# In the scan parts of a hybrid attention and RWKV-7 kernel that keep both directions in one PSUM bank, all products are issued ahead of the reads of the bank

## The chip, the cores and the metric

The kernel runs on one core of one Trainium2 chip. The metric is the time of one execution on the device in microseconds (us). The engines are TensorE (PE, its weight loads PEld), VectorE (DVE), ScalarE (ACT), GpSimd (POOL) and SyncE (SP, which issues most transfers). PSUM is the memory that TensorE writes its products to; a tile of 128 partitions by 512 float32 fills one bank of it.

## What is computed

One layer of an encoder with 2048 tokens of width 1024: a shared input projection, an attention branch (8 heads, low-rank queries and keys), a bidirectional RWKV-7 branch, gates, and a mixture of experts. The change lies in the RWKV-7 branch, a linear recurrence that runs once forward and once backward over the tokens:

```
def step(state, inp):
    r_t, w_t, k_t, v_t, a_t, b_t = inp
    sa = jnp.einsum('bhvk,bhk->bhv', state, a_t)
    state = (state * w_t[:, :, None, :] + sa[..., None] * b_t[:, :, None, :]
             + v_t[..., None] * k_t[:, :, None, :])
    return state, jnp.einsum('bhvk,bhk->bhv', state, r_t)
...
y_f = wkv7_scan(r_h, decay_h[:, :, 0], k_dir[:, :, 0], v_h, -kk, kk * a_h[:, :, 0])
y_b = fl(wkv7_scan(fl(r_h), fl(decay_h[:, :, 1]), fl(k_dir[:, :, 1]), fl(v_h),
                   fl(-kk), fl(kk * a_h[:, :, 1])))
y = y_f + y_b
```

## The kernel before, in words

The program has three phases. Phase 1 projects and prepares the operands. Phase 2, which the change touches, runs attention and both scans interleaved. Phase 3 merges the branches and runs the experts.

The scans cut the 2048 tokens into 32 chunks of 64 (index n). At step n the forward scan works on chunk n and the backward scan on chunk 31 - n; d is the direction. A chunk is worked off in parts, each a method of the class `Rwkv`, and each part's products of both directions go to the two halves of one PSUM bank:

- `products(n, d)` (L968) multiplies keys and receptances within a chunk into the bank `sa`; VectorE masks the result into the tile `stk` (L970). It has one direction to itself.
- `tokens(n, e)` (L990) transposes decayed operands through `sa`; ScalarE copies them to `bkt` (L991).
- `inner(n)` (L1003): 16 products into `sa`, 8 for each direction; VectorE masks each half into `arb` (L1004).
- `state(n)` (L1030): 16 products of the state `mv` into the bank `rec`; ScalarE copies each half to `rs` (L1031). VectorE and GpSimd make the decayed state `m0` from `mv` (L1034). Sixteen products into the bank `yy` follow (L1040).
- `solve(n)` (L1053): 16 products of `rs` with the inverted matrices `tt` into `rec`; of each half VectorE copies the lower 64 partitions back to `mv` (L1055) and ScalarE the upper 64 (L1056).
- `update(n)` (L1069): 16 products into `rec`; VectorE adds `m0` to each half in two instructions, which gives the next state `mv` (L1072). Sixteen products into `yy` follow (L1078), which ScalarE copies to `ys` (L1085).

In `inner`, `state`, `solve` and `update` the products of direction 0 come first, then the reads of its half, then the products and the reads of direction 1. The banks `sa`, `rec` and `yy` have one buffer each.

Attention works on 32 blocks (8 heads by 4 blocks of 512 queries), in four rounds v each. A round issues two times `scores` (four score tiles `s`, each three products of 128x512, L684 to L686, whose exponential ScalarE takes into `e`, L689; VectorE or GpSimd adds `e` to a sum, L694). Between these stand the products of a later block's row maxima (L664), which VectorE reduces (L665). Then comes one step of the scans, then `av` (L701: four products of `e` with the values; in the first round of a block those of the block before), then another step of the scans. So a scan part is followed by `av` in one half of the cases and by a burst of scores in the other. The tiles `s` rotate over four PSUM banks. ScalarE also casts the keys of each new head (`kh`, in the helper `split`, L498) behind the transfer that brings them.

TensorE's order in this phase is that of the code: the loop stands under `tc.manual_schedule(engines={nc.tensor.engine})`. The order on the other engines is made by the tile framework's scheduler, which also puts in the semaphores: it keeps any two engines from working on one PSUM tile at a time, halves included. Each engine works off its own queue in order.

Of the kernel before, what the change touches and what calls it, by code (L numbers as in the profile page):

```python
# [798 lines left out]
class Rwkv:  # L799
# [193 lines left out]
    def inner(self, n):  # L993

        nc = self.k.nc
        st, bk, _ = self.pair[n // 2]
        ar = self.ops[n][0] = self.p.tile([128, 2, 4, 64], F32, name="arb")
        tv = self.bank("sa").rearrange("p (q t) -> p q t", t=64)
        for d in range(2):
            c, s = self.where(n, d)  # L1000
            for g in range(4):
                for e, r, ro in self.HEADS:
                    nc.tensor.matmul(tv[r, 4 * d + g], bk[r, s, d, g, e], st[r, s, e, d, g, 1], start=True, stop=True)  # L1003
            nc.vector.tensor_tensor(ar[:, d], tv[:, 4 * d:4 * d + 4],  # L1004
                                    self.mask[:, d:d + 1, 64:128].to_broadcast([128, 4, 64]), op=OP.mult)

# [5 lines left out]
    def state(self, n):  # L1012

        k, p = self.k, self.p
        nc, Q = k.nc, self.Q
        st, _, mv = self.pair[n // 2]
        if n == 0:
            for e, r, _ in self.HEADS:
                for d in range(2):
                    nc.gpsimd.memset(mv[r, self.where(n, d)[1], e, d], 0.0)  # L1020

        m0 = self.m0 = p.tile([128, 8, 64], F32, name="m0", bufs=1)
        rs = self.rs = p.tile([128, 8, 64], F32, name="rs", bufs=1)
        t, y = self.wide("rec"), self.wide("yy")
        self.y = y
        for d in range(2):
            c, s = self.where(n, d)
            for g in range(4):
                for e, r, _ in self.HEADS:
                    nc.tensor.matmul(t[r, 4 * d + g], st[:, s, e, d, g, 0], mv[:, s, e, d, g], start=True, stop=True)  # L1030
            nc.scalar.copy(rs[:, Q[d]], t[:, Q[d]])  # L1031
            if n < 31:
                for e, r, _ in self.HEADS:
                    (nc.gpsimd if e else nc.vector).tensor_tensor(  # L1034
                        m0[r, Q[d]], mv[r, s, e, d], k.wc[r, d, :, c:c + 1].to_broadcast([64, 4, 64]), op=OP.mult)
        for d in range(2):
            c, s = self.where(n, d)
            for g in range(4):
                for e, r, _ in self.HEADS:
                    nc.tensor.matmul(y[r, 4 * d + g], st[:, s, e, d, g, 1], mv[:, s, e, d, g],  # L1040
                                     start=(d == 0 and g == 0), stop=False)

    def solve(self, n):

        nc, Q = self.k.nc, self.Q
        mv, tt = self.pair[n // 2][2], self.tt[n // 4]
        i = n % 4
        t = self.wide("rec")
        for d in range(2):
            c, s = self.where(n, d)  # L1050
            for g in range(4):
                for e, r, _ in self.HEADS:
                    nc.tensor.matmul(t[r, 4 * d + g], tt[r, d, g, i if d == 0 else 3 - i], self.rs[r, 4 * d + g],  # L1053
                                     start=True, stop=True)
            nc.vector.tensor_copy(mv[self.E, s, 0, d], t[self.E, Q[d]])  # L1055
            nc.scalar.copy(mv[self.O, s, 1, d], t[self.O, Q[d]])  # L1056

    def update(self, n):

        nc, S, Q = self.k.nc, self.k.scratch, self.Q  # L1060
        mv = self.pair[n // 2][2]
        ar, bt = self.ops.pop(n)
        if n < 31:
            t = self.wide("rec")
            for d in range(2):
                c, s = self.where(n, d)
                for g in range(4):
                    for e, r, _ in self.HEADS:
                        nc.tensor.matmul(t[r, 4 * d + g], bt[:, e, 4 * d + g], mv[:, s, e, d, g], start=True, stop=True)  # L1069
                mn, sn = self.pair[(n + 1) // 2][2], self.where(n + 1, d)[1]  # L1070
                for e, r, _ in self.HEADS:
                    nc.vector.tensor_tensor(mn[r, sn, e, d], t[r, Q[d]], self.m0[r, Q[d]], op=OP.add)  # L1072
        y = self.y
        for d in range(2):
            c, s = self.where(n, d)
            for g in range(4):
                for e, r, _ in self.HEADS:
                    nc.tensor.matmul(y[r, 4 * d + g], ar[r, d, g], mv[r, s, e, d, g], start=False,  # L1078
                                     stop=(d == 1 and g == 3))
        if n % 2 == 0:  # L1080
            self.ys = self.p.tile([128, 2, 2, 4, 64], F32, name="ys", bufs=1)
        ys = self.ys
        for d in range(2):
            c, s = self.where(n, d)
            nc.scalar.copy(ys[:, d, s], y[:, Q[d]])  # L1085
            if n % 2:
                c0 = n - 1 if d == 0 else 31 - n
                for e, r, _ in self.HEADS:
                    nc.sync.dma_start(S["y"][d, c0 * 64:c0 * 64 + 128, e * 256:e * 256 + 256]
                                      .rearrange("(c t) x -> t c x", t=64),  # L1090
                                      ys[r, d].rearrange("p s g f -> p s (g f)"))
# [839 lines left out]
```

## Time and profile before

| | us |
|---|---|
| median of 3 runs | 3733.64 (3726.69 to 3735.77) |
| the profiled execution, its own time | 3723.98 |
| its span, first to last instruction | 3722.2 |
| TensorE busy | 3297.7 |
| VectorE busy | 2590.2 |
| ScalarE busy | 1508.5 |
| GpSimd busy | 1399.6 |

The scans' products run from 1327.9 us to 2530.3 us of the span. In a profile, a group's idle time is that of its engine just before the group's instructions, and the arrow behind it names what ended the idle time. The products of a scan part are float32 and are recorded twice each, so that a half of 8 products shows as x16. The end of a product is modelled: a product that runs behind others is shown longer than it holds the engine up, so the starts of consecutive groups tell more than their lengths.

### The profile page before, as it was taken

Reading aid. Unit: us, or ns where it says so; the run is one execution under the profiler, and the core shown is the slowest. Engines: PE = TensorE matmul, PEld = TensorE weight load, DVE = VectorE, ACT = ScalarE, POOL = GpSimd, SP = SyncE. Lnnn points to the kernel's source line nnn. Section 1 sums busy time; section 2 is a strip of 40 time slices with the busy share of each in tenths; the row PEclk is TensorE's granted clock in tenths of the full one; section 3 lists DMA queues with packets and bytes.
Section 4 is the critical chain, followed back from the end, with each engine's and each line's share of the span. In section 5 each row is a group of like instructions: output and inputs, shape, how many; then the busy total and the mean of one; then the engine's idle time right before and its main releaser. Section 6 shows DMA issues by size and latency. Waiting matters only on the chain. (4 is left out here: it accounts for less than half of the span.)

```text
span 3722.2 us, 66958 instructions
## 1 busy us (share of the span) xinstructions
PE 3297.7 (89%) x25104; PEld 2447.8 (66%) x25104; DVE 2590.2 (70%) x4767; ACT 1508.5 (41%) x2866; POOL 1399.6 (38%) x1301
## 2 busy tenths in 40 slices
PE   8999999999888788888888888889699997899990
PEld 6778777777666656555565656565488886666660
DVE  6845677777987656666666666767667676678777
ACT  5322445445443333333333333334322222677762
POOL 1022232234222433444444444434433222565553
PEclk9999999999998889999999999999799998899995
DMA  5545767676554342233332332201454444788887
GB/s 174 167 154 172 214 201 206 199 199 203 193 168 148 118 116 70 65 96 93 89 94 87 90 93 74 62 18 32 130 171 137 131 143 171 260 319 325 335 330 293
DMA packets 392838, 589.71 MB, mean 158 GB/s; under 512 B 66880, under 2 KB 245184, under 8 KB 392512
## 3 DMA queue, kind: packets, MB, share of 16 engines
q1 hardware_dynamic: 380016, 546.36, 46.3%
q0 software_dynamic: 11920, 38.30, 2.7%
q8 instruction: 198, 3.24, 0.4%
q14 instruction: 128, 1.05, 0.1%
q10 hardware_dynamic: 576, 0.76, 0.1%
HBM read 380.78 MB, written 204.51 MB: 157 GB/s over the span
## 5 line engine op out<-in xcount | busy, mean ns | idle before, releaser
L145 PE MATMUL z<-hhi,wlo 128*128 128x512 f32 (+1 forms) x1184 | 469.6, 397 | 4.0 <-POOL wlo L136 4.0
L144 PE MATMUL z<-hlo,whi 128*128 128x512 f32 (+1 forms) x1184 | 471.5, 398 | 0.2 <-DVE hlo L188 0.2
L143 PE MATMUL z<-hhi,whi 128*128 128x512 f32 (+1 forms) x1184 | 469.0, 397 | 1.9 <-ACT hhi L187 1.8
L689 ACT ACTIVATE e<-s 128x512 f32<-128x512 f32 x512 | 304.4, 597 | 393.6 <-PE s L686 370.1
L694 POOL TENSOR_TENSOR acc<-acc,e 128x512 f32<-128x512 f32 x224 | 294.3, 1314 | 403.4 <-ACT e L689 399.4
L665 DVE TENSOR_REDUCE mx<-s 128x1 f32<-128x512 f32 x512 | 339.9, 683 | 82.5 <-PE s L664 80.4
L694 DVE TENSOR_TENSOR accv<-accv,e 128x512 f32<-128x512 f32 x224 | 242.3, 1082 | 41.0 <-ACT e L689 39.3
L136 POOL TENSOR_TENSOR wlo<-wraw,whi 128x1024 fp32r<-128x1024 f32 x61 | 151.4, 2483 | 308.0 <-ACT whi L135 264.1
L145 PEld LDWEIGHTS z<-hhi,wlo 128*128 128x128 f32 (+1 forms) x1184 | 222.7, 188 | 63.6 <-issue 8.8
L144 PEld LDWEIGHTS z<-hlo,whi 128*128 128x128 f32 (+1 forms) x1184 | 222.6, 188 | 56.3 <-issue 3.9
L143 PEld LDWEIGHTS z<-hhi,whi 128*128 128x128 f32 (+1 forms) x1184 | 222.5, 188 | 56.2 <-issue 3.0
L701 PE MATMUL o<-e,v 128*64 128x512 f32 x1024 | 256.4, 623 | 0.0
L498 ACT CAST wh<-wr 128x1024 fp32r<-128x1024 f32 x198 | 204.3, 1047 | 107.1 <-PE y L1632 51.5
L499 POOL TENSOR_TENSOR wl<-wr,wh 128x1024 fp32r<-128x1024 f32 x70 | 186.8, 2687 | 125.9 <-ACT wh L498 125.9
L684 PE MATMUL s<-qhi,kh 128*128 128x512 f32 x512 | 212.4, 415 | 19.8 <-ACT e L689 16.7
L499 DVE TENSOR_TENSOR wl<-wr,wh 128x1024 fp32r<-128x1024 f32 x128 | 185.5, 1455 | 63.0 <-ACT wh L498 58.5
L664 PE MATMUL s<-kh,qhi 128*128 128x512 f32 x512 | 224.0, 445 | 2.2 <-DVE mx L665 2.2
L685 PE MATMUL s<-qlo,kh 128*128 128x512 f32 x512 | 205.9, 402 | 0.0
L686 PE MATMUL s<-qhi,kl 128*128 128x512 f32 x512 | 204.9, 400 | 0.0
L970 DVE TENSOR_TENSOR stk<-sa,mask 64x512 f32<-64x512 f32 x128 | 88.2, 689 | 77.0 <-PE sa L968 75.0
L684 PEld LDWEIGHTS s<-qhi,kh 128*128 128x128 f32 x512 | 98.8, 193 | 59.0 <-ACT e L689 32.7
L664 PEld LDWEIGHTS s<-kh,qhi 128*128 128x128 f32 x512 | 100.9, 198 | 50.6 <-DVE mx L665 11.5
(484 smaller groups left out, 7896.1 us busy)
## 6 DMA issues: line engine op xcount, KB each, us to landing
wr<-w_exp SPq DMA_DIRECT2D x198, 512.0 KB
wraw<-w_in SPq DMA_DIRECT2D x61, 512.0 KB
s_ye<-ye SPq DMA_DIRECT2D x33, 512.0 KB
s_ar<-ar SPq DMA_DIRECT2D x64, 256.0 KB
s_bk<-bk SPq DMA_DIRECT2D x64, 256.0 KB
s_zg<-zo SPq DMA_DIRECT2D x64, 256.0 KB
bk<-s_bk SPq DMA_DIRECT2D x32, 512.0 KB
stk<-s_ar SPq DMA_DIRECT2D x64, 256.0 KB
```

The lines of the kernel that those rows point to most:

```text
L143: nc.tensor.matmul(t[:rows], hi[:, c, :rows], hhi[b][:, c], start=(c == 0), stop=False)
L144: nc.tensor.matmul(t[:rows], hi[:, c, :rows], hlo[b][:, c], start=False, stop=False)
L145: nc.tensor.matmul(t[:rows], lo[:, c, :rows], hhi[b][:, c], start=False, stop=(c == 7))
L499: (eng or k.nc.vector).tensor_tensor(lo, src, hi.bitcast(F32), op=OP.subtract)
L664: nc.tensor.matmul(t, B.qhi[:, i * 128:(i + 1) * 128], KT[B.h][0][b], start=True, stop=True)
L665: nc.vector.tensor_reduce(B.mx[:, i, b:b + 1], t, axis=AX.X, op=OP.max)
L684: nc.tensor.matmul(t, khi[b][:, c], B.qhi, start=True, stop=False)
L685: nc.tensor.matmul(t, khi[b][:, c], B.qlo, start=False, stop=False)
L686: nc.tensor.matmul(t, klo[b][:, c], B.qhi, start=False, stop=True)
L689: nc.scalar.activation(e, t, AF.Exp, scale=scale)
L694: eng.tensor_tensor(a, a, e, op=OP.add)
L701: nc.tensor.matmul(B.o[r], VT[B.h][:, 2 * u + i], B.e[u][i], start=(u == 0), stop=(u == NT // 2 - 1))
```

## The change

In the four parts whose bank holds both directions, the loop over the directions is cut in two: the first loop issues the 16 products, the second the reads of both halves. No instruction is added or removed. TensorE's order is the same instruction by instruction; its waits within a part are gone, and the scheduler orders the other engines anew.

```diff
@@ inner
                 for e, r, ro in self.HEADS:
                     nc.tensor.matmul(tv[r, 4 * d + g], bk[r, s, d, g, e], st[r, s, e, d, g, 1], start=True, stop=True)
+
+        for d in range(2):
             nc.vector.tensor_tensor(ar[:, d], tv[:, 4 * d:4 * d + 4],
                                     self.mask[:, d:d + 1, 64:128].to_broadcast([128, 4, 64]), op=OP.mult)
@@ state
                 for e, r, _ in self.HEADS:
                     nc.tensor.matmul(t[r, 4 * d + g], st[:, s, e, d, g, 0], mv[:, s, e, d, g], start=True, stop=True)
+        for d in range(2):
+            c, s = self.where(n, d)
             nc.scalar.copy(rs[:, Q[d]], t[:, Q[d]])
@@ solve
                     nc.tensor.matmul(t[r, 4 * d + g], tt[r, d, g, i if d == 0 else 3 - i], self.rs[r, 4 * d + g],
                                      start=True, stop=True)
+        for d in range(2):
+            c, s = self.where(n, d)
             nc.vector.tensor_copy(mv[self.E, s, 0, d], t[self.E, Q[d]])
             nc.scalar.copy(mv[self.O, s, 1, d], t[self.O, Q[d]])
@@ update
                     for e, r, _ in self.HEADS:
                         nc.tensor.matmul(t[r, 4 * d + g], bt[:, e, 4 * d + g], mv[:, s, e, d, g], start=True, stop=True)
+            for d in range(2):
                 mn, sn = self.pair[(n + 1) // 2][2], self.where(n + 1, d)[1]
                 for e, r, _ in self.HEADS:
                     nc.vector.tensor_tensor(mn[r, sn, e, d], t[r, Q[d]], self.m0[r, Q[d]], op=OP.add)
```

With the change L1004, L1031, L1053, L1055, L1056, L1069, L1072 and L1078 become L1006, L1035, L1057, L1061, L1062, L1075, L1079 and L1085.

TensorE around the update and the inner part behind it, at n = 1, before:

```order
L716 MATMUL s<-cst,acc 128x2 x3
L1069 MATMUL rec<-mv,bkt 64x64 x8
L1069 MATMUL rec<-mv,bkt 64x64 [waits DVE_49]
L1069 MATMUL rec<-mv,bkt 64x64 x7
L1078 MATMUL yy<-mv,arb 64x64 x16
L701 MATMUL o<-e,v 64x512 x4
L1003 MATMUL sa<-stk,bk 64x64 x8
L1003 MATMUL sa<-stk,bk 64x64 [waits DVE_49]
L1003 MATMUL sa<-stk,bk 64x64 x7
```

and with the change:

```order
L716 MATMUL s<-cst,acc 128x2 x3
L1075 MATMUL rec<-mv,bkt 64x64 x16
L1085 MATMUL yy<-mv,arb 64x64 x16
L701 MATMUL o<-e,v 64x512 x4
L1003 MATMUL sa<-stk,bk 64x64 x16
```

The two waits on VectorE in the middle of a part are gone, and nothing stands in another place.

VectorE around the solve part of n = 2 (`mv<-rec` is its copy of a half, L665 the maxima of a burst of scores), before:

```order
L707 TENSOR_TENSOR ob<-o,ob 64x512 [waits DMAHW1_49,Activation_49]
L1055 COPY mv<-rec 64x256 [waits PE_49]
L1055 COPY mv<-rec 64x256 [waits PE_49,Activation_49]
L665 TENSOR_REDUCE mx<-s 128x1 [waits PE_49] x3
L694 TENSOR_TENSOR accv<-accv,e 128x512 [waits DVE_49,Activation_49]
L665 TENSOR_REDUCE mx<-s 128x1 [waits PE_49]
```

and with the change:

```order
L707 TENSOR_TENSOR ob<-o,ob 64x512 [waits DMAHW1_49,Activation_49]
L1061 COPY mv<-rec 64x256 [waits PE_49]
L665 TENSOR_REDUCE mx<-s 128x1 [waits PE_49]
L1061 COPY mv<-rec 64x256 [waits Activation_49]
L665 TENSOR_REDUCE mx<-s 128x1 [waits PE_49] x2
L694 TENSOR_TENSOR accv<-accv,e 128x512 [waits DVE_49,Activation_49]
L665 TENSOR_REDUCE mx<-s 128x1 [waits PE_49]
```

The second copy no longer waits for products of its own but for ScalarE, which reads the same bank between the two, and one of the maxima has moved ahead of it.

ScalarE around the same solve part (L991 is the copy of the transposed tokens, whose products follow the solve on TensorE), before:

```order
L706 COPY ob<-o 64x512 [waits DMAHW1_49,PE_49,Pool_49]
L1056 COPY mv<-rec 64x256 [waits DVE_49]
L991 COPY bkt<-sa 128x512 [waits PE_49]
L1056 COPY mv<-rec 64x256 [waits DVE_49]
L689 ACTIVATE e<-s 128x512 [waits PE_49,Activation_49]
L689 ACTIVATE e<-s 128x512 [waits PE_49,Pool_49]
L689 ACTIVATE e<-s 128x512 [waits PE_49,Activation_49]
L689 ACTIVATE e<-s 128x512 [waits PE_49,Pool_49]
```

and with the change:

```order
L706 COPY ob<-o 64x512 [waits DMAHW1_49,PE_49,Pool_49]
L991 COPY bkt<-sa 128x512 [waits PE_49]
L1062 COPY mv<-rec 64x256 [waits DVE_49]
L689 ACTIVATE e<-s 128x512 [waits PE_49,Activation_49]
L1062 COPY mv<-rec 64x256 [waits DVE_49]
L689 ACTIVATE e<-s 128x512 [waits PE_49,Activation_49] x2
L689 ACTIVATE e<-s 128x512 [waits PE_49,Pool_49]
```

The copy L991 has moved ahead of the first of the two copies of the solve, and an exponential ahead of the second.

## Rows read from the trace of the kernel before

**Rows 1.** Windows with and without scans: busy us by engine, granted clock, DMA.

```profile
1600.00:1800.00 200.00, 175.01 (x1724) 119.68 (x1722) 132.25 (x205) 68.79 (x130) 84.56 (x83) 0.96 0.33 92
...
2560.00:2600.00 40.00, 38.88 (x173) 22.65 (x172) 33.15 (x46) 16.62 (x29) 20.12 (x17) 1.00 0.06 14
```

**Rows 2.** Waits of TensorE over the span: total us, times, longest.

```profile
PE rec L1053 <- ACT mv L1056: 46.7, 32, 4.8
PE rec L1069 <- DVE mv L1072: 46.7, 31, 2.6
PE sa L1003 <- DVE arb L1004: 26.5, 32, 3.4
PE rec L1030 <- ACT rs L1031: 17.4, 32, 0.9
PE s L684 <- ACT e L689: 16.7, 22, 3.0
...
PE s L664 <- DVE mx L665: 2.2, 4, 1.1
```

**Rows 3.** The same for TensorE's weight loads.

```profile
PEld rec L1053 <- ACT mv L1056: 51.1, 32, 4.9
PEld rec L1069 <- DVE mv L1072: 51.0, 31, 2.8
...
PEld sa L1003 <- DVE arb L1004: 30.9, 32, 3.5
...
PEld rec L1030 <- ACT rs L1031: 21.8, 32, 1.0
```

**Rows 4.** Timeline, all engines, one update part and the scores behind it.

```profile
1967.19 0.64 PE L1069 MATMUL rec<-mv,bkt 128*64 128x64 f32 x16
...
1967.87 0.88 DVE L1072 TENSOR_TENSOR mv<-rec,m 64x256 f32<-64x256 f32 x2 [1.96 <-PE rec L1069]
...
1968.80 0.69 PE L1069 MATMUL rec<-mv,bkt 128*64 128x64 f32 x16 [0.98 <-DVE mv L1072]
1969.42 1.15 PE L1078 MATMUL yy<-mv,arb 64*64 64x64 f32 x32
...
1970.44 1.18 DVE L1034 TENSOR_TENSOR m<-mv,wc 64x256 f32<-64x256 f32 x2
...
1970.88 0.48 PE L664 MATMUL s<-kh,qhi 128*128 128x512 f32 x1
...
1975.37 0.68 PE L1003 MATMUL sa<-stk,bk 64*64 64x64 f32 x16
```

**Rows 5.** Timeline of TensorE: two other bursts of scores, first and next group.

```profile
1904.81 0.51 PE L664 MATMUL s<-kh,qhi 128*128 128x512 f32 x1
...
1909.12 0.69 PE L1030 MATMUL rec<-mv,stk 128*64 128x64 f32 x16
...
1926.24 0.48 PE L664 MATMUL s<-kh,qhi 128*128 128x512 f32 x1
...
1930.21 0.69 PE L1069 MATMUL rec<-mv,bkt 128*64 128x64 f32 x16
```

**Rows 6.** Windows: the first and the last of 18 stretches at half clock.

```profile
1391.90:1395.30 3.40, 3.40 (x50) 2.57 (x46) 2.02 (x4) 0.65 (x2) 1.55 (x2) 0.50 0.02 5
2504.60:2508.00 3.40, 3.40 (x36) 2.99 (x35) 1.51 (x3) 0.65 (x2) 0.00 (x0) 0.51 0.01 2
```

**Rows 7.** Timeline of TensorE at the first of these stretches.

```profile
1391.64 0.94 PE L1069 MATMUL rec<-mv,bkt 128*64 128x64 f32 x16 [1.17 <-DVE mv L1072]
1392.51 1.97 PE L1078 MATMUL yy<-mv,arb 64*64 64x64 f32 x32
```

**Rows 8.** Groups by line, 1345:2530 (busy us, mean ns, idle before).

```profile
L991 ACT COPY bkt<-sa 128x512 f32<-128x512 f32 x62 | 36.3, 585 | 54.1 <-PE sa L990 53.5
...
L1055 DVE COPY mv<-rec 64x256 f32<-64x256 f32 x63 | 25.9, 410 | 39.0 <-PE rec L1053 39.0
...
L498 ACT CAST kh<-raw 96x512 fp32r<-96x512 f32 x24 | 14.8, 617 | 44.0 <-DMA raw<-s_krr 44.0
```

## The prediction

> **What bounds the kernel now.** I read the windows first. With scans running, TensorE is busy 175 of 200 us, VectorE 132, ScalarE 69 and GpSimd 85, at a granted clock of 0.96; in the stretch of attention behind the last scan part TensorE is busy 38.9 of 40 us at a clock of 1.00 [rows 1]. So the stage with scans, some 1,200 of 3,722 us, is TensorE's, and one eighth of it is lost to waits that attention alone does not have. The list of TensorE's waits names them: the second half of a solve waits 46.7 us in all for ScalarE's copy, that of an update 46.7 us for VectorE's sums, that of an inner part 26.5 us for the mask, that of a state part 17.4 us for the copy to `rs`. That is 137.3 us in 127 waits. The next ones on the list in this stage are small: 16.7 us for the exponential to give back a score bank, 2.2 us for a maximum [rows 2]. TensorE's order is fixed in the code, so nothing else can be put into these holes: what one costs is lost to the whole stage, and the stage is passed before phase 3 can go on.
>
> **The change, part by part.** Nothing is added or removed; what moves are waits.
>
> *The waits inside the parts.* All 127 go: the 16 products stand in one piece. In the timeline of one update the second half starts 1.61 us behind the first (1967.19 to 1968.80), while the second half hands over to the next line after 0.62 us; the idle time printed between them is 0.98 us [rows 4]. The idle of a matmul counts from a modelled end. The weight loads, which the same waits hold back, show 51.1 + 51.0 + 30.9 + 21.8 = 154.8 us [rows 3]. The gain lies between 137.3 and 154.8 us; I take 150, nearer to the loads, because a load is what has to start first.
>
> *The clock.* Between 1345 and 2530 us the trace has 18 stretches at a granted clock of half (1.2 GHz), 15 of 3.4 us and 3 of 6.8 us; the first and the last are shown [rows 6]. Sixteen of them, 14 short and 2 long, begin within 6 us of the start of one of the waits that go, of 1.2 to 4.8 us [rows 2, 7]; the other two begin behind waits for an exponential, of up to 3.0 us [rows 2]. In the first one 32 products take 1.97 us [rows 7], which take 1.15 us at full clock [rows 4]. The 16 sum to 14 x 3.4 + 2 x 6.8 = 61 us, of which half, 31 us, is lost where TensorE is busy all along. Some of it passes in idle, and a new wait can bring a stretch back: I take 22, with 0 and 31 as ends.
> The Trainium skill (TensorE: Matmul & The Clock Gate, "A second HAM failure mode: psum-queue depth-cycling") says that short idles between groups of matmuls, which come from cycling through PSUM, make the clock fall and rise again and again. The trace agrees as far as 16 of 18 stretches go. If the whole stage kept its clock by this rule, half of 71 us would come back, and the sum would be 14 us lower.
>
> *What comes instead, behind the parts.* Two engines read what TensorE has left, and now begin behind all 16 products. Where `av` follows (half of the cases), it covers them. Where a burst of scores follows, the maxima stand behind the reads in VectorE's queue, and the four score banks run out. Two bursts give the price: one behind transposed tokens takes 3.97 us (1926.24 to 1930.21), one behind `products`, a part whose reads already begin behind all of its products, 4.31 us [rows 5]: 0.34 us more. Behind an update a burst takes 4.49 us already (1970.88 to 1975.37), and one pair of sums of 0.88 us, now done inside the wait, will stand ahead of it too, with the 1.18 us of the next `m0` behind as now [rows 4]. So 16 updates at up to 0.88 us give 14 us, 16 inner parts at 0.34 give 5, and 16 solves at 0.34 give 5; the two copies of a state part are covered by the products into `yy` (1.15 us for 32, as in rows 4's update). Sum 24; between 5 (the sums covered by the `yy` products) and twice that.
>
> *The backlog.* Of the 137.3 us a part was not the read itself but an engine that was late. The least price of an update's wait is its two sums and 0.10 us of handing over, 0.98 [rows 4]; 31 of them are 30.4 of 46.7. A solve needs two copies of about 0.41 us [rows 8], one behind the other, and two hand-overs, 1.02; 32 are 32.6 of 46.7. An inner or state part needs one, 0.51: 16.3 of 26.5 and of 17.4. That leaves 16.3 + 14.1 + 10.2 + 1.1 = 42 us of lateness, which does not vanish: it meets `av` in one half of the cases and the four score banks in the other. I let a third return, 14, with 0 and 42 as ends.
>
> *The casts.* ScalarE stands 44.0 us behind transfers before it casts the keys of a new head [rows 8]; TensorE feels part of that as its 16.7 us. The transfers will not be faster, and TensorE arrives at them sooner: 8 us more, between 0 and 27 (44.0 less 16.7).
>
> *The sum.* 3724.0 (the profiled execution's own time; its span is 3722.2) - 150 - 22 + 24 + 14 + 8 = 3598. The median of the runs, 3733.6, lies 9.7 above that execution, so the forecast for the median is 3608, 3.4% less. Taking every term at its better end gives 154.8 + 31 - 5 = 181 less, 3553; at its worse end 137.3 - 48 - 42 - 27 = 20 less, 3713. Phases 1 and 3 keep their order on every engine and are costed at nothing: the first product that changes lies at 1328 us, and the last difference on any engine lies ahead of the merge.
>
> **Rivals.**
> *A. The bursts take most of it.* VectorE's 132 us of 200 [rows 1] become about 78% if the stage loses 172 of 1,200 us, and it is unevenly loaded: it is late at the end of a burst and catches up behind it. The holes that go are where it caught up. If it no longer does, each of the some 112 bursts beside the 224 scan steps pays about 0.7 us more (twice the 0.34 behind `products`): 80 us, so 3688. For it speaks that bursts already stretch from 3.97 to 4.49 us; against it that only 2.2 us of waiting for maxima stand in the list [rows 2], and that `av` lies between any two bursts.
> The Trainium skill (Perfetto Trace Analysis, "Optimizing Tensor Performance", "Matmuls") wants independent groups in different banks, so that the reads of one lie beside the products of the next. The change does the contrary within a part, and by this rule rival A, with its 3688, is the likelier one. The trace bears it out only where a burst follows, since `av` and the bursts use other banks than the part.
> *B. Nothing changes.* Each wait reappears whole at the next semaphore, for the score banks or for `sa`: 3733. For it speaks that the same engines still have to read the same halves. Against it: behind each part stands `av` or a burst, and neither uses the bank that is being read.
> *C. Slower: the alternation of VectorE and ScalarE in the solve.* With the change VectorE's second copy waits for ScalarE's first one, and ScalarE has the tokens' copy L991 (0.585 us [rows 8]) ahead of that, in all 32 solves. An engine that is stuck there keeps maxima and exponentials behind it in its queue, and TensorE runs out of score banks. It decides once a solve costs TensorE over 172 / 32 = 5.4 us; at 6 us the time is 3733.6 - 172 + 192 = 3754. The chain itself is only 4 x 0.41 + 0.59 = 2.2 us, so that would need a cast that waits for its transfer in most solves, where there are 24 casts.
>
> **How the numbers follow.** My sum 0.77, A 0.15, B 0.05, C 0.03. The range leaves C and B out and reaches into A: 3565 to 3690; the likeliest case's own is 3575 to 3645. Differences under 0.3% can't be told from no change here. Faster 0.92, same 0.05, slower 0.03.
>
> **What would show it.** Right: the four waits in rows 2 are gone; in the windows TensorE is busy over 190 of 200 us with a clock of 0.98 or more; at most three or four of the 16 stretches at half clock remain; waits for score banks, 18.9 us today, rise to some 40 to 70; the last scan product comes near 2,400 us instead of 2,530. Wrong: waits for maxima or exponentials over 100 us (A), waits of VectorE for ScalarE's copy in the solve that end on TensorE (C), or a clock that stays at 0.97 although the waits are gone, which would strike the term of 22.

## The result, and the profile after

The changed kernel takes 3568.6 us (3562.3 to 3569.7, 4 runs) against 3732.6 us: a ratio of 0.9559 (0.9542 to 0.9575), 164 us less. Timed twice more beside other kernels the ratio was 0.9547 (0.9528 to 0.9565) and 0.9556 (0.9543 to 0.9569). The profiled execution took 3567.97 us at a span of 3566.2 us.

The waits of TensorE in the changed kernel (total us, times, longest); those left out belong to phases 1 and 3 or are under 4 us:

```profile
PE s L684 <- ACT e L689: 21.7, 25, 2.6
...
PE s L684 <- DVE mx L665: 12.0, 13, 2.9
...
PE s L664 <- DVE mx L665: 4.7, 6, 1.1
...
PE s L684 <- DVE ob L727: 3.0, 3, 1.0
```

The four rows that stood at the head of [rows 2] have no successor. Waits for the four score banks are 41.4 us now. They were 18.9 us in [rows 2], and 20.7 with a row that is not shown there:

```profile
PE s L684 <- DVE mx L665: 1.8, 1, 1.8
```

VectorE's maxima have become nearly as frequent a cause (19 waits) as ScalarE's exponentials (25).

Windows with scans and, last, without them:

```profile
1600.00:1800.00 200.00, 190.16 (x2018) 131.37 (x2018) 155.19 (x241) 81.11 (x155) 103.27 (x101) 1.00 0.38 107
...
2000.00:2200.00 200.00, 189.67 (x1989) 131.75 (x1986) 152.57 (x239) 78.00 (x149) 96.00 (x91) 0.97 0.33 91
...
2420.00:2460.00 40.00, 40.00 (x182) 24.34 (x182) 28.97 (x40) 18.10 (x31) 20.32 (x16) 1.00 0.06 14
```

TensorE is busy 190 of 200 us where [rows 1] had 175, VectorE 155 where it had 132, and the granted clock is 1.00 in the first of these stretches, 0.97 in the second. The last product of the scans starts at 2368.3 us; it started at 2530.3 us. The stage from the first to the last product of the scans' bank `rec` went from 1197.2 to 1035.1 us, 162 us less, and what lies behind it, which the change does not touch, is 6 us longer in this profile.

Timeline of the same update as in [rows 4] (n = 16) and of the burst behind it, TensorE and VectorE:

```profile
1876.86 1.10 PE L1075 MATMUL rec<-mv,bkt 128*64 128x64 f32 x32
...
1877.89 1.15 PE L1085 MATMUL yy<-mv,arb 64*64 64x64 f32 x32
1878.01 1.75 DVE L1079 TENSOR_TENSOR mv<-rec,m 64x256 f32<-64x256 f32 x4 [2.42 <-PE rec L1075]
...
1878.97 0.62 PE L725 MATMUL s<-cst,rd 128*64 128x128 f32 x4
...
1879.35 0.48 PE L664 MATMUL s<-kh,qhi 128*128 128x512 f32 x1
...
1879.79 1.18 DVE L1038 TENSOR_TENSOR m<-mv,wc 64x256 f32<-64x256 f32 x2
...
1881.00 0.68 DVE L727 TENSOR_TENSOR ob<-s,ob 64x512 f32<-64x512 f32 x1
...
1881.61 2.06 DVE L665 TENSOR_REDUCE mx<-s 128x1 f32<-128x512 f32 x3
...
1881.74 0.50 PE L684 MATMUL s<-qhi,kh 128*128 128x512 f32 x1 [0.98 <-DVE ob L727]
...
1884.49 0.68 PE L1003 MATMUL sa<-stk,bk 64*64 64x64 f32 x16
```

The part hands over to the products into `yy` 1.03 us behind its start, where it took 2.23 us [rows 4]. VectorE's four sums (1.75 us) and `m0` (1.18 us) now lie in one piece behind it. The four score banks are meanwhile used up: one by products that finish an earlier block of attention (L725), three by the burst. TensorE stands 0.98 us until VectorE, behind `m0`, has read the first of them (L727, which ends at 1881.68); the maxima begin only then. The burst takes 5.14 us (1879.35 to 1884.49), where it took 4.49 us [rows 4]. So 1.20 us are gained in the part and 0.65 us given back behind it.

The same read over the whole stage, from the starts of products in the two traces:

| | before | after |
|---|---|---|
| 32 solves, first product to the next line, sum of us | 90.1 | 36.7 |
| 31 updates | 86.8 | 32.7 |
| 32 inner parts | 69.3 | 36.4 |
| 32 state parts | 56.2 | 31.4 |
| bursts, starts of neighbouring products beyond the undisturbed 0.23 us, stretches at half clock left out | 50.7 | 77.9 |
| of these, bursts behind updates | 9.2 | 19.2 |
| behind inner parts | 3.3 | 7.5 |
| behind state parts | 2.4 | 5.7 |
| behind tokens, after a solve | 5.5 | 14.2 |
| behind `products`, which the change leaves alone | 24.2 | 23.7 |
| us at half clock between 1345 us and the last scan product | 71.7 | 10.2 |

The parts lose 165.2 us and the bursts get 27.2 back; 25.7 of these stand in the five rows named. The stage is 162.1 us shorter, so 24 us are left for the clock.

This remainder can be read another way. `av`, the tokens and the products into `yy` keep their work and their place; by the starts of products they took 320.6 us before, 36.2 of them at half clock, and 308.1 after, 5.3 of them at half clock. That is 12.5 us less for 30.9 us less at half clock, 0.40 for each. Of the parts' own time 12.8 us lay at half clock before and 3.7 after, so up to 4.5 of the 165.2 us are the clock's as well.

### The profile page after: what moved, and what is told of

It reads as the page before. It is cut to its first block, busy times and chain, and to the rows that moved or that the text cites. A ratio compares the mean times of both kernels' runs of the same rounds, so it can differ in the third digit from the quotient of the medians.

```text
span 3566.2 us, 66955 instructions
## 1 busy us (share of the span) xinstructions
PE 3245.5 (91%) x25104; PEld 2414.4 (68%) x25104; DVE 2593.4 (73%) x4767; ACT 1505.7 (42%) x2866; POOL 1400.6 (39%) x1301
## 5 line engine op out<-in xcount | busy, mean ns | idle before, releaser
L665 DVE TENSOR_REDUCE mx<-s 128x1 f32<-128x512 f32 x512 | 337.4, 682 | 46.6 <-PE s L664 44.4
L684 PE MATMUL s<-qhi,kh 128*128 128x512 f32 x512 | 210.6, 411 | 38.7 <-ACT e L689 21.7
```

Source lines behind the costliest of these rows:

```text
L665: nc.vector.tensor_reduce(B.mx[:, i, b:b + 1], t, axis=AX.X, op=OP.max)
L684: nc.tensor.matmul(t, khi[b][:, c], B.qhi, start=True, stop=False)
```

## The experiments

My theory at this point: the time is that of the waits inside the parts, plus a return of the clock, minus new waits for score banks. Its rivals: the waits move on, so that only the last one undone pays; the clock's fall has another cause or costs nothing; and what came back is ScalarE's and VectorE's ordinary lateness.

**One part at a time.** `e1_solve` has the diff's third piece alone, `e2_update` the fourth, `e3_inner_state` the first two.

> Only the solve part is split, the three others stay as before. Theory (TensorE's waits in the part go, with the half-clock stretches that follow them, and a little comes back as waits for score banks): the weight loads' wait of 51.1 us goes; 9 of the 16 half-clock stretches stand behind a solve's wait (7 of 3.4 and 2 of 6.8 us, half of 37.4 is 18.7 us); about 9 us come back in the bursts behind. So 61 us less than before, near 3672. Rival (the wait moves on to the next semaphore, and only the last of several undone waits pays): under 25 us less.

> Only the update part is split. Theory: the loads' wait of 51.0 us goes, 6 short half-clock stretches (half of 20.4 is 10.2 us) go with it, 10 us come back in the bursts behind: 51 us less than before, near 3682. Rival (VectorE's sums pile up ahead of the maxima and take most of it): under 25 us less.

> Only the inner and the state parts are split. Theory: the loads' waits of 30.9 and 21.8 us go, one half-clock stretch (1.7 us) goes, 7 us come back: 47 us less than before, near 3685. With the two others 159 us, so the three sum to the 164 of the whole change; under the rival that the wait moves on, the three sum to much less than the whole.

| | median us | ratio to before | stage, us less | us at half clock, less |
|---|---|---|---|---|
| e1_solve | 3680.9 | 0.9854 (0.9835 to 0.9873) | 44.6 | 10.3 |
| e2_update | 3684.4 | 0.9872 (0.9853 to 0.9890) | 47.4 | 10.3 |
| e3_inner_state | 3671.8 | 0.9845 (0.9828 to 0.9862) | 64.3 | 16.6 |
| all, the changed kernel | 3568.6 | 0.9559 (0.9542 to 0.9575) | 162.1 | 61.5 |

The three ratios leave 1.46 + 1.28 + 1.55 = 4.3% beside 4.4% for the whole: the parts add within the intervals (the three together to 0.3), and the rival that waits move on falls. The waits of `e1_solve` show it directly:

```profile
PE rec L1071 <- DVE mv L1074: 51.1, 31, 2.8
PE sa L1003 <- DVE arb L1004: 24.6, 32, 1.8
PE s L684 <- ACT e L689: 20.5, 24, 3.5
PE rec L1030 <- ACT rs L1031: 17.4, 32, 0.9
```

The solve's row is gone, and the three others stand where they stood in [rows 2], 46.7, 26.5 and 17.4 us, within 5 us. The single expectations were less good: e1 was to give 61 us and gave 52, e2 51 and gave 48, e3 was to give 47 and gave 61.

Each expectation had handed a half-clock stretch to the part in front of it. The profiles speak against that: time at half clock goes down by 10 to 17 us for one part and by 61.5 us for all of them, and in `e1_solve`, which should have left 9 stretches, 14 begin, behind waits that remain. But these are single profiles, and the three of the changed kernel have 10.2, 17.1 and 17.1 us. The granted clock of every run, over the whole execution, gives 24, 22 and 22 us less for the three parts, with standard errors of 6 to 11, and 68 to 82 less for all of them, which is no more than the sum. That mending one part brings back less of the clock than its share is therefore not shown.

**The clock by itself.** Both kernels keep the order and the waits of before; extra products, whose results nobody reads, fill the middle of each solve and update.

```diff
+    def fill(self, mm):
+        v = self.wide("sa")
+        for g in range(6):
+            for e, r, _ in self.HEADS:
+                mm(v, r, g % 4)
...
             nc.vector.tensor_copy(mv[self.E, s, 0, d], t[self.E, Q[d]])
             nc.scalar.copy(mv[self.O, s, 1, d], t[self.O, Q[d]])
+            if d == 0:
+                self.fill(lambda v, r, g: nc.tensor.matmul(v[r, g], tt[r, 0, g, i], self.rs[r, g],
+                                                           start=True, stop=True))
```

`update` gets the like, from its own operands `ar` and `mv`. `e4_filler` has 24 such products in each place, `e9_filler12` the 12 of this diff.

> The kernel before, in its own order, with 24 extra products of 64x64 into the free bank sa in the middle of each solve and update, behind the products of direction 0 (their result is not read). They take some 0.7 us, and each of these waits lasts at least 0.9 us, so the waits stay, but TensorE works through most of them. Theory that the half-clock stretches are due to TensorE standing still there and cost half of their length: most of the 15 behind solves and updates go, the mean clock of the stage rises from 0.97 to 0.99, and the time falls by 15 to 29 us. Rival (the falls of the clock have another cause, or cost nothing since TensorE is waiting anyway): no change, or a few us slower for the extra products.

The ratio was 0.9983 (0.9973 to 0.9993), 6 us less, with 30.7 us at half clock instead of 71.7. My filler was too long: 24 products took 1.6 us, not 0.7 (a half of 8 products is recorded as x16, and I had taken the records for products). Solves and updates grew from 90.1 to 93.3 and from 86.8 to 100.0 us, 16 us in all, which ate most of the gain. So I halved it:

> The kernel before with 12 extra products in place of the 24, some 0.8 us with their hand-over, so that they end ahead of every read they stand beside (the 24 took 1.6 us and stretched the solves by 3 and the updates by 13 us in all). Theory (time at half clock costs half of its length in this stage): the solves and updates last as long as before (90.1 and 86.8 us from first product to the next line), about half to two thirds of the 71.7 us at half clock go, and the time falls by half of that, 18 to 24 us. If TensorE stands still long enough in what is left of the longer waits, fewer stretches go; the time should then still fall by half of what goes. Rival (half clock costs nothing here, since TensorE waits for others): no change.

The ratio was 0.9959 (0.9946 to 0.9973): 3714.3 against 3728.5 us, 14 us less. Timeline of TensorE around an update of this kernel:

```profile
1389.82 0.69 PE L1079 MATMUL rec<-mv,bkt 128*64 128x64 f32 x16
1390.43 0.92 PE L1085 MATMUL sa<-mv,arb 64*64 64x64 f32 x24
1391.66 0.69 PE L1079 MATMUL rec<-mv,bkt 128*64 128x64 f32 x16 [0.31 <-DVE mv L1082]
1392.28 1.15 PE L1092 MATMUL yy<-mv,arb 64*64 64x64 f32 x32
1393.36 1.94 PE L701 MATMUL o<-e,v 128*64 128x512 f32 x8
```

The filler (L1085, 0.92 us) ends ahead of VectorE's sums, and the second half still waits 0.31 us. It starts 1.84 us behind the first, as it did without the filler, where it started 1.85 us behind (1391.64 in [rows 7]) this group of the kernel before:

```profile
1389.79 0.69 PE L1069 MATMUL rec<-mv,bkt 128*64 128x64 f32 x16
```

Solves sum to 91.1 and updates to 88.0 us, 2 us more than before. In [rows 7] the 32 products into `yy` behind the same update took 1.97 us; here they take 1.15. The stage of before and, in the second row, of this kernel:

```profile
1345.00:2530.00 1185.00, 1029.81 (x10398) 709.05 (x10400) 791.60 (x1245) 417.19 (x789) 506.13 (x474) 0.97 0.27 75
```

```profile
1345.00:2515.00 1170.00, 1062.30 (x11920) 741.83 (x11916) 789.66 (x1245) 417.42 (x789) 506.24 (x474) 0.99 0.27 76
```

The mean granted clock goes from 0.97 to 0.99. Time at half clock is 30.7 us as in e4, 41 less, and the stage 14.9 us shorter. With the 2 us of the parts that is 0.36 to 0.42 us of time for each us at half clock, where I had expected a half. `e4_filler`, read in the same way, gives more: its stage is 4.6 us shorter with 16.4 us lost in the parts, 21 us for 41, or 0.5. With the 0.40 of `av`, the tokens and `yy` above, some 0.4 is the best reading. The rival that the clock costs nothing falls, and so does another cause than TensorE's standing still: the waits are all still there, only filled.

**What came back, and whether it can be had.** The change left two kinds of waits, for maxima and for exponentials. Three kernels move work away from or to the place that I suspected, and `e5_merged` shortens the reads. `e8_after` and `e12_after` are the changed kernel again, as marks on the same chip.

> The changed kernel again, as the mark for the three runs beside it: 164 us less than before, as measured.

> The changed kernel a third time, as the mark for the two runs on m0 and the casts beside it: 164 to 170 us less than before, as in its two timings so far.

They gave 3560.7 us against 3730.4 and 3564.6 us against 3728.5.

In `e5_merged` the inner part has one mask of 128x512 and the state part one copy:

```diff
-        for d in range(2):
-            nc.vector.tensor_tensor(ar[:, d], tv[:, 4 * d:4 * d + 4],
-                                    self.mask[:, d:d + 1, 64:128].to_broadcast([128, 4, 64]), op=OP.mult)
+        nc.vector.tensor_tensor(ar, tv.rearrange("p (d g) t -> p d g t", d=2),
+                                self.mask[:, :, 64:128].rearrange("p d (o t) -> p d o t", o=1)
+                                .to_broadcast([128, 2, 4, 64]), op=OP.mult)
...
-            nc.scalar.copy(rs[:, Q[d]], t[:, Q[d]])
+        nc.scalar.copy(rs, t)
```

> The changed kernel with one read instead of two in the inner part (a mask of 128x512 on VectorE) and in the state part (a copy of 128x512 on ScalarE). Theory that what came back is reads standing ahead of maxima and exponentials in their queues: the reads shorten from 0.83 to about 0.69 and from 0.74 to 0.585 us, the bursts behind these parts, which wait 7.5 and 5.7 us more than an undisturbed one, give back some 3 us: 2 to 5 us less than the changed kernel. Rival: no difference, since av covers them.

Its ratio was 0.9563 (0.9546 to 0.9581) beside 0.9547 (0.9528 to 0.9565) for e8_after: no difference that these runs can tell. In the trace the bursts behind inner parts wait 6.3 us instead of 7.5, those behind state parts 6.2 instead of 5.7. The 2 to 5 us that were expected did not show, and whether the reads of these two parts set the waits behind them stays open.

In `e6_m0_pool` and `e11_m0_dve` the line `(nc.gpsimd if e else nc.vector).tensor_tensor(` of `m0` becomes `nc.gpsimd.tensor_tensor(` and `nc.vector.tensor_tensor(`.

> The changed kernel with all of the decayed state m0 made on GpSimd, half of which VectorE made before. VectorE's 1.2 us between an update's sums and the maxima of a burst goes. Theory (the bursts behind updates wait 1.2 us each, 19 us in all, because VectorE is not yet free): 8 to 12 us less than the changed kernel, and the waits for maxima about halved from their 17 us. Rival (GpSimd, now with 3.1 us of m0 a chunk, delays the sums of exponentials or the next update): same or slower.

> The changed kernel with all of m0 on VectorE: 1.3 us more between an update's sums and the maxima of the burst behind. Theory that VectorE's queue at that place sets the waits for maxima: the 16 bursts behind updates wait 1.2 us more each, up to 20 us in all, and the time rises by 10 to 20 us. Rival (the four score banks and av absorb it): under 5 us more.

Timeline of e6, the burst behind the same update:

```profile
1871.98 1.75 DVE L1079 TENSOR_TENSOR mv<-rec,m 64x256 f32<-64x256 f32 x4 [2.42 <-PE rec L1075]
...
1873.32 0.48 PE L664 MATMUL s<-kh,qhi 128*128 128x512 f32 x1
...
1873.76 0.68 DVE L727 TENSOR_TENSOR ob<-s,ob 64x512 f32<-64x512 f32 x1
...
1877.47 1.15 PE L1003 MATMUL sa<-stk,bk 64*64 64x64 f32 x32
```

and of e11:

```profile
1888.28 0.48 PE L664 MATMUL s<-kh,qhi 128*128 128x512 f32 x1
...
1888.70 1.72 DVE L1038 TENSOR_TENSOR m<-mv,wc 64x256 f32<-64x256 f32 x4
...
1893.62 1.09 PE L1003 MATMUL sa<-stk,bk 64*64 64x64 f32 x30
```

The burst takes 4.15 us (1873.32 to 1877.47) without `m0` on VectorE and 5.34 us (1888.28 to 1893.62) with all of it, beside 5.14 in the changed kernel. Over all bursts behind updates the wait is 3.5, 19.2 and 28.9 us. The time follows: e11 has a ratio of 0.9603 (0.9583 to 0.9623) beside 0.9556 (0.9543 to 0.9569) for e12_after, 16 us more; e6 0.9534 (0.9513 to 0.9555) beside 0.9547 (0.9528 to 0.9565) for e8_after, 4 us less where 8 to 12 were expected, which the runs alone do not settle; in the profiles its stage is 11 us shorter (1025.6 against 1036.5). VectorE's queue ahead of the maxima sets these waits behind updates. The rival that `av` and the banks absorb it falls for e11.

In `e7_cast_pool` the keys' cast leaves ScalarE:

```diff
-                split(k, hi[0:96], lo[0:96], raw, nc.gpsimd)
+                nc.gpsimd.tensor_copy(hi[0:96], raw)
+                nc.gpsimd.tensor_tensor(lo[0:96], raw, hi[0:96].bitcast(F32), op=OP.subtract)
```

> The changed kernel with the cast of a new head's keys made on GpSimd instead of ScalarE. Theory that TensorE's waits for exponentials (21.7 us) come from ScalarE standing behind these transfers: they fall to some 8 us, and the time by 8 to 15 us against the changed kernel. Rival (they are the ordinary lateness of ScalarE in a burst): the waits stay, and the time within 3 us of the changed kernel, or above it since GpSimd now stands behind the transfers with its sums.

Timeline of the changed kernel at one such cast, ScalarE and TensorE:

```profile
2102.40 0.62 ACT L498 CAST kh<-raw 96x512 fp32r<-96x512 f32 x1 [3.66 <-DMA raw<-s_krr]
2102.92 1.07 ACT L689 ACTIVATE e<-s 128x512 f32<-128x512 f32 x2
...
2103.56 0.80 PE L684 MATMUL s<-qhi,kh 128*128 128x512 f32 x1 [2.64 <-ACT e L689]
```

and its window just behind:

```profile
2103.30:2113.50 10.20, 9.94 (x62) 6.57 (x63) 4.75 (x6) 2.61 (x6) 2.29 (x2) 0.50 0.42 120
```

ScalarE stands 3.66 us behind the transfer of `raw`; two exponentials that were ready follow it, TensorE stands 2.64 us for a score bank, and the clock is at half for 10.2 us: all of the half-clock time left in the stage in this profile. In the profiles of e8_after and e12_after it is 17.1 us each, behind waits in bursts too. The waits of e7 (its lines are one further down):

```profile
PE s L685 <- DVE mx L666: 11.8, 13, 3.2
PE s L665 <- DVE mx L666: 9.6, 6, 4.5
PE s L685 <- ACT e L690: 7.3, 15, 0.5
```

Waits for exponentials fall from 21.6 us in e8_after to 7.3; those for maxima rise from 16.5 to 21.4. Its ratio was 0.9527 (0.9508 to 0.9546), 8 us less than e8_after, again not settled by the runs alone; its stage is 15 us shorter (1021.5 us). So I ran both moves together:

> The changed kernel with both moves to GpSimd, all of m0 and the casts of the keys. In the profiles the one shortened the stage from the first to the last product of the scans by 11 us, the other by 15 us against the changed kernel. Theory (two separate lots of waits, for maxima and for exponentials): they add, 20 to 26 us less than the changed kernel, near 3540. Rival (GpSimd, which then has both, becomes late for the sums that give the tiles e back, or for m0): under 10 us less.

The ratio was 0.9488 (0.9475 to 0.9501), beside 0.9556 (0.9543 to 0.9569) for e12_after: 3537.5 us, 27 us less than the changed kernel and 191 us less than the one before. This is the fastest version here. Its waits for score banks and one window of its stage:

```profile
PE s L665 <- DVE mx L666: 8.9, 4, 4.6
PE s L685 <- ACT e L690: 7.3, 15, 0.5
PE s L685 <- DVE mx L666: 6.4, 5, 2.9
```

```profile
1600.00:1800.00 200.00, 196.96 (x2100) 137.84 (x2098) 151.86 (x240) 82.25 (x157) 119.63 (x121) 1.00 0.39 109
```

TensorE is busy 197 of 200 us. GpSimd went from 103 to 120 us, and no wait of TensorE of over 1 us in this stage names it. By the profiles the two moves add (stages 11 and 15 us shorter alone, 33 together, 1005.9 against 1038.5 in e12_after), and that rival falls. The medians of the single moves, 4 and 8 us, are too rough to add up.

## Why the prediction was right, and where its sizes were off

Forecast were 3608 us, 126 less, in a range of 3565 to 3690; measured were 3568.6, 164 less. The mechanism was the one forecast; its sum was 38 us too small. The time lies only 4 us inside the range, and it is outside the 3575 to 3645 that I had given for my own case: it was the wider range that held it.

The terms were read from the profiled executions, 3724.0 and 3568.0 us, and there the sum, 3598, was 30 us too high. The terms below were 36 us off (15 + 2 - 3 + 14 + 8), and 6 us went the other way behind the scans, where I had put nothing. The other 8 to 9 us lie between the profiled executions and the medians: that of before was 9.7 us faster than its median, that of the changed kernel 0.6.

**The waits inside the parts** were taken at 150 us, between 137.3 and 154.8. They were worth 165, over my better end; this term is the largest error of size. Up to 4.5 of the 165 are the clock's, so some 6 us or more were missing from the idle of the weight loads too: by the starts of products an update lost (86.8 - 32.7) / 31 = 1.75 us, by the loads' idle 51.0 / 31 = 1.65. The parts add, as e1 to e3 show.

**The clock** was taken at 22 us and gave about 24 (what the stage has left over) or, at e9's price of 0.36 to 0.42 us for each of 61.5 us, 22 to 26. Here the size was right: 61 us at half their length, less something for idle, is 22, and that "something" was a guess that e9's price bears out. By the profiles of e1 to e3 the handing of stretches to single parts did not hold. The Trainium skill (TensorE: Matmul & The Clock Gate, "A second HAM failure mode: psum-queue depth-cycling") names short idles around PSUM as what makes the clock fall. The trace agrees, with 16 of 18 stretches behind the waits in the parts, and e9 shows it from the other side: filled with idle work, the same waits bring the clock down less (30.7 us at half instead of 71.7). That all of the half-clock time would come back, 14 us beyond my sum, did not happen; a cast's wait kept 10.2 us of it.

**Behind the parts** I had 24 us and measured 27: updates 10.0 of 14, inner parts 4.2 of 5, solves 8.7 of 5, state parts 3.3 where I had none. That VectorE's work ahead of the maxima is the cause is shown by e6 and e11 for the bursts behind updates; for the others it is likely and not shown.

**The backlog and the casts**, 14 and 8 us, are the step that failed. I had counted lateness that would return in the bursts beside the reads: 24 + 14 + 8 = 46 us in all. The bursts pay 27 for all three together, and how these divide between reads and lateness the runs do not tell, beyond the updates. The bursts behind `products` wait as long as before (23.7 and 24.2 us), so no lateness was carried on into those. An engine that was late has, it seems, until the next burst or longer to catch up; that is argued, not shown. Waits for exponentials rose by 5 us only, from 16.7 to 21.7. That most of them came from casts was right, as e7 shows (21.6 us fall to 7.3), and that they would grow by much was wrong.

**Rival A** priced VectorE's unevenness at 80 us on top. VectorE is busy 155 of 200 us, as it said, and pays 27 in all. The Trainium skill (Perfetto Trace Analysis, "Optimizing Tensor Performance", "Matmuls") wants groups in different banks so that reads lie beside products; here both groups stay in one bank, and the reads lie beside the products that follow, which use another one. The trace is on the rule's side only in the 27 us. **Rival B** is refuted by e1 to e3. **Rival C** is there and harmless: VectorE's wait for ScalarE's copy in the solve,

```profile
DVE mv L1061 <- ACT mv L1062: 9.8, 12, 1.6
```

0.3 us a solve where it would have taken 5.4 to decide.

What the profile was to show came out nearly as said: the four rows gone, TensorE busy 190 us of 200 (189.7 at a clock of 0.97 in the second window above, where over 190 and 0.98 were forecast), waits for score banks of 41.4 us (40 to 70 forecast), and none of the 16 stretches left. The last scan product at 2368 us came earlier than the 2,400 I had named.

## What to carry to other kernels

Where two independent groups of products share a PSUM bank and the scheduler lets no two engines into a bank at once, issue both groups before the first read, if other work for TensorE stands behind them in another bank: each hand-over in the middle cost 0.8 (state part) to 1.75 us (update) here, and the reads can lie beside what follows. Price such a wait by the starts of the products with and without it, not by the printed idle time (165 against 137 us here). Then look at what stands ahead in the reading engine's queue of that which frees the next banks, and move it, and any instruction that waits for a transfer, to an engine that TensorE does not wait for.

## What was not expected of the hardware

Time at half clock follows TensorE's standing still: in the profiles, mending all four parts took 61.5 of 71.7 us away, and filling two of the four with unread products, with their waits in place, 41. In this stage, where TensorE sets the pace, a us at half clock cost some 0.4 us (0.36 to 0.5 by the readings above). And extra work on the engine that bounds the kernel made it 14 us faster.
